# Second-layer tokens stored before their norm, and modulation pieces computed in column groups between stages

## The chip, the cores and the metric

One core of a Trainium2 chip runs the whole program in one launch. The metric is device time in microseconds: three runs gave 3576.17, 3576.55 and 3577.59, median 3576.55. The profile comes from one further execution.

## What is computed

Two transformer blocks on 512 latent tokens of width 1024, all in float32. The first block has two layers and 256 context tokens beside the latent ones; the second block has one layer and is untouched by the change. A layer of the first block:

```python
mod = silu_c @ w_ada[l] + b_ada[l]            # six pieces of 1024
sh1, sc1, gt1, sh2, sc2, gt2 = split(mod, 6)  # modc: the same from c_ctx
h = modulate(rmsnorm(x, g_mix[l]), sh1, sc1)
x = x + gt1 * latent_mixer(h @ w_in[l], ...)  # attention, conv, gates, w_branch, w_out
h2 = modulate(rmsnorm(x, g_ffn[l]), sh2, sc2)
x = x + gt2 * expert_choice_ffn(h2, w_router[l], w_e_gate[l], w_e_up[l], w_e_down[l])
```

`expert_choice_ffn` takes a softmax over 16 experts for every token; each expert then picks its 64 best tokens (32 of the context), applies a gated network of width 1024 and adds the result, times its affinity, to the rows it took. In layer 0 the context tokens go through the same; in layer 1 they only give keys and values.

## The kernel before

Activations lie transposed in SBUF, features on the partitions (8 x 128) and tokens in the free dimension. A dense product takes its weights in blocks of 0.5 MB (`weights`, L86): SP issues the load into `raw`, ScalarE makes a rounded float32r copy `wh` (L95), VectorE the rest `wl` (L96), and TensorE runs three float32r products per block of 128 features (`mm3`, L80, lines L82 to L84). `w` pools hold so many `raw` and so many `wh`/`wl` buffers: 2 and 3 in the latent mixers; 3 and 3 in the context mixer, which has a second pool `w1` with 2 and 2 and takes the two in turn.

**Order.** The stages are: first layer's latent mixer (to about 660 us), context mixer (to 917), first layer's experts (948 to 1600), second layer's latent mixer (to 2180), second layer's experts (2222 to about 2680), second block. In a mixer (`mixer`, L799) dense work and attention are interleaved by hand (`weave`), and at ticks between dense steps a `background` list is advanced (`step`, L411; `period` is the number of ticks per advance). A scheduler then fixes the order on every engine and queue from estimated times, the program's order being its priority, so an instruction that is ready early can stand ahead of earlier ones. Queues then run in order. SBUF of a closed pool is taken over by later ones, tile by tile, and the first user waits for the last reader.

**Modulation.** `first_ada` (L462) computes pieces 0 and 1 of layer 0 at the start in float32: the two condition vectors as 2-column stationary, 256 columns of `w_ada` at a time, with four `wada` buffers; every product is two records in the trace. `ada` (L428) computes the other pieces in the background with split weights: 8 blocks of 0.5 MB a piece, on each four pairs of float32r products (L441, L442), and after every second block a row copy (L444) and two small transposes (L447). The latent mixers do pieces 2 to 5 of their layer, the context mixer pieces 0 and 1 of layer 1. The latent mixer of layer 0 also has `first_gather` (L492), an indirect load into a dummy tile, in its background.

**From w_out to the experts.** During w_out `residual` (L926) makes each 128 features of the new x, and `put` (L963) squares them, scales them by the norm's gain into `u` and adds their part of the router's logits (L970). `ffn_input` (L936) has before that spread the shift `sh2` over all partitions by diagonal products (L954, L955) into `row`. `finish` (L973) sums the squares over features (L979), takes the inverse root on GpSimd (L242), the softmax, and `top_k` (L1019) on VectorE. It then transposes `u` into token rows (L1002), scales them by the norm, adds `row` and writes them to `h2d` in DRAM (L1015). In layer 1 ScalarE scales (L1013) and GpSimd adds (L1014).

**Experts of layer 1** (`last_experts`, L1244) stream 192 blocks of 1 MB (L1269) through 18 buffers, `era` (8) and `erb` (10), on the right side of SBUF where the dense stage's pools lay. The products (`product`, L1265) are float32 with 64 tokens as stationary, the two halves of the columns in the two column groups of TensorE (L1273). `pair` (L1277) gathers the rows of two experts from `h2d` (128 rows, two buffers) and transposes them (L1287). Layer 0's experts (`experts`, L1095) use split weights, five raw buffers, and gather at L1140.

## Time and profile before

| | before |
|---|---|
| median of three runs | 3576.55 us |
| profiled execution | 3583.02 us (span 3581.3) |
| PE busy | 3354.1 us, 94% |
| DVE / ACT / POOL busy | 2268.4 / 1732.4 / 274.4 us |
| granted TensorE clock, mean | 0.977 |
| DMA | 732.9 MB, 205 GB/s over the span |

PE is TensorE's matmuls, DVE VectorE, ACT ScalarE, POOL GpSimd, SP the engine whose queue issues most loads; a "q" behind an engine is its instruction queue. A matmul's recorded length includes its way through the array, so the distance between starts is its price, and a busy PE need not be at its peak.

### The profile page before, as it was taken

The page shows a single profiled execution, that of the slowest core. Times are in us where ns is not written, and L with a number is a line of the kernel's source. Part 1 is how long each engine was busy: PE and PEld are TensorE (multiplying, and loading weights), DVE is VectorE, ACT ScalarE, POOL GpSimd, SP SyncE. Part 2 cuts the span into 40 slices and gives each one's busy share as a digit, 9 for nine tenths or more (in the row PEclk, how much of TensorE's full clock was granted, in tenths as well). Part 3 has the DMA queues.
Part 4 walks back from the last instruction along what each step waited for, and adds up shares of the span by engine and source line. Part 5 has one row for each costly group of instructions (what it writes and reads, how often), then busy time and mean ns, then how long its engine had stood idle before and what let it go on. Part 6 is the DMA issues. An engine that isn't in the chain of part 4 may idle for free. (4 is left out here: it accounts for less than half of the span.)

```text
span 3581.3 us, 46471 instructions
## 1 busy us (share of the span) xinstructions
PE 3354.1 (94%) x17762; PEld 2572.3 (72%) x17762; DVE 2268.4 (63%) x3543; ACT 1732.4 (48%) x2542; POOL 274.4 (8%) x322
## 2 busy tenths in 40 slices
PE   8999999999799999989999996998889999989998
PEld 5787777898688888877777774332228887768887
DVE  4787676588599999977776753232235456854444
ACT  3555554456477777745555542110115355633333
POOL 1101110000200000021011101000001000010000
PEclk9999999999899999989999997999999999999999
DMA  6332437458799999933334376999993432244332
GB/s 218 119 100 93 135 122 220 145 168 239 269 373 335 367 339 341 350 127 95 100 101 130 121 235 255 421 421 421 421 367 103 128 87 88 84 130 138 100 94 83
DMA packets 369227, 732.90 MB, mean 205 GB/s; under 512 B 25534, under 2 KB 262060, under 8 KB 342636
## 3 DMA queue, kind: packets, MB, share of 16 engines
q1 hardware_dynamic: 355728, 695.15, 55.1%
q0 software_dynamic: 7184, 33.31, 2.4%
q8 instruction: 140, 2.29, 0.3%
q10 hardware_dynamic: 6092, 1.47, 0.2%
q14 instruction: 83, 0.68, 0.1%
HBM read 683.71 MB, written 46.14 MB: 204 GB/s over the span
## 5 line engine op out<-in xcount | busy, mean ns | idle before, releaser
L96 DVE TENSOR_TENSOR wl<-raw,wh 128x1024 fp32r<-128x1024 f32 (+2 forms) x423 | 506.6, 1200 | 370.6 <-ACT wh L95 362.9
L95 ACT ACTIVATE wh<-raw 128x1024 fp32r<-128x1024 f32 (+2 forms) x423 | 436.6, 1034 | 490.4 <-PE d L83 301.0
L82 PE MATMUL d<-hh,wh 128*128 128x512 f32 (+1 forms) x1304 | 485.4, 373 | 5.5 <-ACT hh L301 4.3
L83 PE MATMUL d<-hl,wh 128*128 128x512 f32 (+1 forms) x1304 | 484.1, 371 | 1.8 <-DVE hl L302 1.6
L84 PE MATMUL d<-hh,wl 128*128 128x512 f32 (+1 forms) x1304 | 484.3, 372 | 0.4 <-DVE wl L96 0.4
L1116 DVE TENSOR_TENSOR el<-eraw,eh 128x2048 fp32r<-128x2048 f32 x192 | 433.8, 2287 | 33.2 <-ACT eh L1115 32.5
L1115 ACT ACTIVATE eh<-eraw 128x2048 fp32r<-128x2048 f32 x192 | 365.3, 1918 | 105.6 <-PE pup L84 39.3
L82 PEld LDWEIGHTS d<-hh,wh 128*128 128x128 f32 x1304 | 247.6, 190 | 44.1 <-ACT hh L301 5.1
L83 PEld LDWEIGHTS d<-hl,wh 128*128 128x128 f32 x1304 | 247.3, 190 | 39.8 <-DVE hl L302 4.6
L84 PEld LDWEIGHTS d<-hh,wl 128*128 128x128 f32 x1304 | 247.3, 190 | 39.2 <-DVE wl L96 2.3
L642 ACT ACTIVATE prob<-S,st 128x768 f32<-128x768 f32 (+3 forms) x176 | 134.5, 764 | 142.2 <-DVE st L640 66.9
L1332 DVE SCALAR_TENSOR_TENSOR y<-pdn,route,y 64x512 fp32r<-64x512 f32 x32 | 24.0, 750 | 280.6 <-ACT y L1331 280.5
L82 PE MATMUL d<-wh,hh 128*128 128x256 f32 (+1 forms) x528 | 161.2, 305 | 1.9 <-ACT hh L301 1.8
L83 PE MATMUL d<-wl,hh 128*128 128x256 f32 (+1 forms) x528 | 159.9, 303 | 0.3 <-DVE wl L96 0.3
L84 PE MATMUL d<-wh,hl 128*128 128x256 f32 (+1 forms) x528 | 159.7, 303 | 0.2 <-DVE hl L302 0.2
L638 DVE TENSOR_REDUCE st<-S 128x1 f32<-128x768 f32 (+3 forms) x176 | 137.2, 783 | 23.5 <-PE S L703 21.3
L658 ACT ACTIVATE pth<-ppt 128x512 fp32r<-128x512 f32 x184 | 106.0, 595 | 74.8 <-PE ppt L655 71.5
L659 DVE TENSOR_TENSOR ptl<-ppt,pth 128x512 fp32r<-128x512 f32 x184 | 122.6, 685 | 27.2 <-ACT pth L658 26.1
L1273 PE MATMUL pdn<-eraw,at 128*64 128x512 f32 x512 | 119.0, 599 | 21.1 <-DMA eraw<-in_w_e_down 16.4
L655 PE MATMUL ppt<-ident,prob 128*128 128x128 f32 x736 | 121.6, 277 | 7.2 <-DVE prob L647 6.6
L1273 PE MATMUL pup<-eraw,xt 128*64 128x512 f32 x512 | 119.9, 600 | 6.0 <-DMA eraw<-in_w_e_up 6.0
L1273 PE MATMUL pga<-eraw,xt 128*64 128x512 f32 x512 | 118.5, 605 | 2.7 <-DMA eraw<-in_w_e_gate 2.7
(546 smaller groups left out, 7596.4 us busy)
## 6 DMA issues: line engine op xcount, KB each, us to landing
eraw<-in_w_e_gate SPq DMA_DIRECT2D x128, 1024.0 KB
eraw<-in_w_e_up SPq DMA_DIRECT2D x128, 1024.0 KB
eraw<-in_w_e_down SPq DMA_DIRECT2D x128, 1024.0 KB
raw<-in_w_in SPq DMA_DIRECT2D x170, 512.0 KB
raw<-in_w_ada SPq DMA_DIRECT2D x80, 512.0 KB
raw<-in_w_ff SPq DMA_DIRECT2D x64, 512.0 KB
raw<-in_w_out SPq DMA_DIRECT2D x32, 512.0 KB
raw<-in_w_branch SPq DMA_DIRECT2D x48, 256.0 KB
```

The lines of the kernel that those rows point to most:

```text
L82: mm(ps, wh, xh, start=first, stop=False, skip_group_check=skip)
L83: mm(ps, wh, xl, start=False, stop=False, skip_group_check=skip)
L84: mm(ps, wl, xh, start=False, stop=last, skip_group_check=skip)
L95: for ins in (nc.scalar.activation(h[:, :n], raw[:, :n], AF.Copy), nc.vector.tensor_sub(l[:, :n], raw[:, :n], h[:, :n])):
L96: nc.vector.tensor_sub(l[:, :n], raw[:, :n], h[:, :n])):
L638: nc.vector.tensor_reduce(nm, S[:, s0:s1], axis=AX, op=ALU.max, negate=True)
L642: nc.scalar.activation(p, S[:, s0:s1], AF.Exp, bias=nm, accum_out=ls)
L655: nc.tensor.transpose(pt[:, h * 128:h * 128 + 128], probs[h], self.ident)
L659: nc.vector.tensor_sub(pl, pt, ph)
L1115: nc.scalar.activation(h, raw, AF.Copy)
L1116: nc.vector.tensor_sub(lo, raw, h)
L1273: nc.tensor.matmul(ps[halves[j], :], x(k), raw[:, i, j * 512:j * 512 + 512], start=k == 0, stop=k == 7, skip_group_check=True)
```

## The change

Five things. (1) In layer 1 the token rows are transposed and written during w_out, after features 0 to 3 and 4 to 7, unscaled, to a new array `h3d` whose rows have 8 more columns for the norm's factor, written in `finish`; `pair` multiplies by a diagonal of that factor where it transposed before, and adds the shift (loaded as columns through DRAM, in the order in which the layer's features lie) on VectorE. The first two experts' rows are gathered apart, 64 and 64, and there is one gather buffer. (2) Pieces 5 of layer 0, 0 and 1 of layer 1 (after the context mixer's w_out) and 5 of layer 1 (after the latent one's) are made by `ada_between` in float32 with 512 columns in each of two column groups; the latent backgrounds keep pieces 2 to 4 with a period of 4 ticks instead of 3. (3) `first_ada` sets its two pieces side by side in the two column groups. (4) The dummy gather goes, and the context mixer's second weight pool, whose place a pool `z` of five 0.5 MB load buffers takes; in layer 1 the loads use the two `qT` buffers. (5) In layer 1 the pool of `u` lies ahead of the weight pool; the norm's sums take another PSUM tile; one context store moves from POOL's queue to ScalarE's.

```diff
         for q in range(4):
-            for p in (1, 0):
-                ps = self.pd.tile([128, 512], F32, name="d", tag="d")[:2, :256]
-                c0 = p * 1024 + q * 256
-                for ch in range(0, 8, 4):
+            ps = self.pd.tile([128, 512], F32, name="d", tag="d")[:, :256]
+            for ch in range(0, 8, 4):
+                ws = []
+                for p in (1, 0):
                     w = raw[:, n % 4].rearrange("p (k f) -> p k f", k=4)
                     n += 1
+                    c0 = p * 1024 + q * 256
                     nc.sync.dma_start(w, self.A["w_ada"][0][ch * 128:ch * 128 + 512, c0:c0 + 256]
                                       .rearrange("(k p) f -> p k f", p=128))
-                    for k in range(4):
-                        nc.tensor.matmul(ps, self.cs[:, ch + k, :], w[:, k], start=ch + k == 0, stop=ch + k == 7)
-                rows = self.tp.tile([4, 256], F32, name="arow", tag="arow", bufs=1)[:2]
-                nc.scalar.activation(rows, ps, AF.Copy)
-                pt = self.pt.tile([128, 512], F32, name="apt", tag="t")
+                    ws.append(w)
+                for k in range(4):
+                    for h, w in zip((0, 64), ws):
+                        nc.tensor.matmul(ps[h:h + 2], self.cs[:, ch + k, :], w[:, k], start=ch + k == 0,
+                                         stop=ch + k == 7, skip_group_check=True)
...
+                nc.scalar.activation(rows[:2, p * 256:p * 256 + 256], ps[h:h + 2], AF.Copy)
+                for j in range(p * 2, p * 2 + 2):
+                    nc.tensor.transpose(pt[:, j * 2:j * 2 + 2], rows[:2, j * 128:j * 128 + 128], self.ident[:2, :2])
+                self.modulation(0, p, pt[:, p * 4:p * 4 + 4], q * 2, 2)
+            yield
+    def ada_between(self, l, p, raw, banks, row):
+        nc = self.nc
+        ps, pt = banks()
+        k = 0
+        while k < 8:
+            w = raw()
+            n = w.shape[1]
+            nc.sync.dma_start(w, self.A["w_ada"][l][k * 128:(k + n) * 128, p * 1024:p * 1024 + 1024]
+                              .rearrange("(i p) f -> p i f", p=128))
+            for i in range(n):
                 for j in range(2):
-                    nc.tensor.transpose(pt[:, j * 2:j * 2 + 2], rows[:, j * 128:j * 128 + 128], self.ident[:2, :2])
-                c = slice(p * 8 + q * 2, p * 8 + q * 2 + 2)
-                b = lambda a: a[:, None, :].to_broadcast([128, 2, 2])
-                nc.vector.tensor_add(mod[:, :, c], pt[:, :4].rearrange("p (j i) -> p i j", i=2), b(vec[:, c]))
-                if p == 1:
-                    nc.vector.tensor_scalar(mod[:, :, c], mod[:, :, c], 1.0, None, ALU.add)
-                    nc.vector.tensor_mul(mod[:, :, c], mod[:, :, c], b(vec[:, 48 + q * 2:50 + q * 2]))
...
-    def first_gather(self):
-        nc.gpsimd.indirect_dma_start(out=t, out_offset=None, in_=self.A["k_ident"],
-                                     in_offset=bass.IndirectOffsetOnAxis(ap=zero[:, 0:1], axis=0))
...
@@ mixer
         self.do(self.fm(self.A["w_out"][l], 8, 0, 1024, mh, ml, T, residual))
+        between()
         finish()
@@ ffn_input, put, finish
-        row = [self.tp.tile([128, 512], F32, name="brow", tag="hn", bufs=4) for _ in range(2)]
-        for hf in range(2):
+        if l == 1:
+            vec = self.dp.tile([D], F32, name="shift")
+            self.shift = self.cp.tile([128, 8], F32, name="shift", tag="hg")
+            nc.gpsimd.dma_start(vec.rearrange("(k p) -> p k", p=128), B)
+            nc.gpsimd.dma_start(self.shift, vec.rearrange("(c p i) -> p c i", c=4, i=2))
+        row = [self.tp.tile([128, 512], F32, name="brow", tag="hn", bufs=4) for _ in range(2)] if l == 0 else []
+        for hf in range(len(row)):
...
+            if l == 1 and j % 4 == 3:
+                tokens(j // 4)
+        def tokens(hf):
+            for t0 in range(0, nt, 2):
+                tok = self.tp.tile([128, 2, 512], F32, name="tok", tag="big", bufs=2)
+                for t in range(2):
+                    ps = self.pt.tile([128, 512], F32, name="hpt", tag="t")
+                    for j in range(4):
+                        nc.tensor.transpose(ps[:, j * 128:j * 128 + 128],
+                                            u[:, hf * 4 + j, (t0 + t) * 128:(t0 + t) * 128 + 128], self.ident)
+                    ov = tok[:, t].rearrange("t (c i p) -> t c i p", c=2, i=2)
+                    pv = ps.rearrange("t (c p i) -> t c i p", c=2, i=2)
+                    if t == 0:
+                        nc.scalar.activation(ov, pv, AF.Copy)
+                    else:
+                        nc.vector.tensor_copy(ov, pv)
+                nc.gpsimd.dma_start(self.h3d[t0 * 128:t0 * 128 + 256, hf * 512:hf * 512 + 512]
+                                    .rearrange("(t p) f -> p t f", p=128), tok)
         def finish():
-            if lat:
-                ps = self.ps.tile([128, 1024], F32, name="S", tag="S")
-            else:
-                ps = self.ps.tile([128, 512], F32, name="S", tag="Sc", bufs=2)
+            ps = self.pd.tile([128, 512], F32, name="nps", tag="d")
...
+            if l == 1:
+                r8 = self.sp.tile([128, 128], F32, name="r8", tag="diag", bufs=2)[:, :32].rearrange("p (t o) -> p t o", o=8)
+                nc.vector.tensor_copy(r8, r[:, :, None].to_broadcast([128, 4, 8]))
+                nc.gpsimd.dma_start(self.h3d[:, D:].rearrange("(t p) o -> p t o", p=128), r8)
...
                     pass
+            if l == 1:
+                return
...
-                    else:
-                        ov = o.rearrange("t (c i p) -> t c i p", c=2, i=2)
-                        pv, rv = (a.rearrange("t (c p i) -> t c i p", c=2, i=2) for a in (ps, row[hf]))
-                        nc.scalar.activation(ov, pv, AF.Copy, scale=r[:, t:t + 1])
-                        nc.gpsimd.tensor_add(ov, ov, rv)
@@ last_experts
-            def pair(n):
-                xs = xp.tile([128, 1024], F32, name="xs", tag="xs")
-                nc.gpsimd.indirect_dma_start(out=xs, out_offset=None, in_=h2d,
-                                             in_offset=bass.IndirectOffsetOnAxis(ap=gidx[:, n:n + 1], axis=0))
+            first = kp.tile([128, 2], U32, name="gfirst")
+            nc.vector.tensor_copy(first, lat[:, 0, 0:2])
+            def pair(n, alone=False):
+                xs = xp.tile([128, D + 8], F32, name="xs", tag="xs", bufs=1)
                 x = xp.tile([128, 8, 128], F32, name="xt", tag="xt")
-                for hf in range(2):
-                    pt = pm.tile([128, 4, 128], F32, name="ept", tag="d", bufs=5)
-                    for j in range(4):
-                        k = hf * 4 + j
-                        nc.tensor.transpose(pt[:, j], xs[:, k * 128:k * 128 + 128], self.ident)
-                    nc.scalar.activation(x[:, hf * 4:hf * 4 + 4], pt, AF.Copy)
-                return [lambda k, h=h: x[:, k, h] for h in halves]
+                parts = halves if alone else (slice(0, 128),)
+                for i, h in enumerate(parts):
+                    idx = first[:64, i:i + 1] if alone else gidx[:, n:n + 1]
+                    nc.gpsimd.indirect_dma_start(out=xs[h], out_offset=None, in_=self.h3d,
+                                                 in_offset=bass.IndirectOffsetOnAxis(ap=idx, axis=0))
+                for h in parts:
+                    rows = xp.tile([128, 128], F32, name="rows", tag="rows")
+                    nc.vector.tensor_scalar(rows[h, h], self.ident[h, h], xs[h, D:D + 1], None, ALU.mult)
+                    for hf in range(2):
+                        pt = pm.tile([128, 4, 128], F32, name="ept", tag="d", bufs=5)
+                        for j in range(4):
+                            k = hf * 4 + j
+                            nc.tensor.matmul(pt[:, j, h], xs[h, k * 128:k * 128 + 128], rows[h, h], start=True, stop=True)
+                        b = self.shift[:, hf * 4:hf * 4 + 4, None].to_broadcast([128, 4, h.stop - h.start])
+                        nc.vector.tensor_add(x[:, hf * 4:hf * 4 + 4, h], pt[:, :, h], b)
+                    xs_all.extend(lambda k, h=g: x[:, k, h] for g in halves if h.start <= g.start < h.stop)
+                    yield
+            xs_all = []
...
-            xs = pair(0)
+            xs = xs_all
+            two = pair(0, True)
+            next(two)
             pga = acc(pa, "pga")
             run(product(pga, xs[0], A["w_e_gate"][l, 0]))
+            next(two)
...
-                    xs += pair(e // 2 + 1)
+                    next(pair(e // 2 + 1))
@@ open_dense, first_block
         self.tp, self.sp = self.pool(es, "tmp", 2), self.pool(es, "small", 4)
+        if outputs:
+            self.op = self.pool(es, "o")
         if not k:
             self.wps = [(self.pool(es, "w", 3), nraw, nw)]
+        self.h3d = dp.tile([TL, D + 8], F32, name="h3d")
...
-                    self.open_dense(e1)
-                    self.hx, self.op = self.pool(e1, "hx"), self.pool(e1, "o")
+                    self.open_dense(e1, outputs=not first)
+                    self.hx = self.pool(e1, "hx")
+                    if first:
+                        self.op = self.pool(e1, "o")
...
-                    self.background, self.ticks, self.period = [self.ada(l, (2, 3, 4, 5))], -6, 3
-                    if first:
-                        self.background.append(self.first_gather())
-                    xL = self.mixer(l, True, hl, xLd, mLd, gLd, kvc, sink, self.xlp, h2d, 0, xL, arrive())
+                    self.background, self.ticks, self.period = [self.ada(l, (2, 3, 4))], -6, 4
+                    def between():
+                        if first:
+                            return
+                        S = self.ps.tile([128, 1024], F32, name="S", tag="S")
+                        self.ada_between(l, 5, lambda: self.ap.tile([128, 4, TL], F32R, name="zraw", tag="qT", bufs=2)
+                                         .rearrange("p (i a) t -> p i (a t)", i=2).bitcast(F32),
+                                         lambda: [S[:, :512], S[:, 512:]],
+                                         lambda: self.pp.tile([128, 512], F32R, name="zrow", tag="pth").bitcast(F32))
+                    xL = self.mixer(l, True, hl, xLd, mLd, gLd, kvc, sink, self.xlp, h2d, 0, xL, arrive(), between)
...
-                        more = self.pool(e1, "w1"), 2, 2
+                        zp = self.pool(e1, "z", 5, side="right")
                         self.open_dense(e1, nraw=3, nw=3, side="right")
-                        self.wps.append(more)
+                        def between():
+                            for m, p in ((0, 5), (1, 0), (1, 1)):
+                                self.ada_between(m, p, lambda: zp.tile([128, 1, 1024], F32, name="zraw", tag="zraw"),
+                                                 lambda: [self.ps.tile([128, 512], F32, name="S", tag="Sc", bufs=2)
+                                                          for _ in range(2)],
+                                                 lambda: zp.tile([128, 512], F32, name="zrow", tag="zrow", bufs=2))
...
-                        self.background = [self.top_k(True, fp), vectors(), self.load_vectors_2(), self.ada(1, (0, 1))]
+                        self.background = [self.top_k(True, fp), vectors(), self.load_vectors_2()]
                         self.ticks, self.period = -15, 2
                         self.nprob = 8
-                        xC = self.mixer(0, False, [hh, hl], xCd, mCd, gCd, kvc, sink, xcp, h2d, TL)
+                        xC = self.mixer(0, False, [hh, hl], xCd, mCd, gCd, kvc, sink, xcp, h2d, TL, between=between)
                         self.drain()
-                        nc.gpsimd.dma_start(xCd, xC)
+                        nc.scalar.dma_start(xCd, xC)
```

## Rows read from the trace of the kernel before

**Rows 1.** Busy time by stage: us of the stretch, engines' busy us, granted clock, DMA share, GB/s.

```profile
core 0: us, PE busy (x) PEld busy (x) DVE busy (x) ACT busy (x) POOL busy (x), PEclk, DMA share, GB/s
130.00:500.00 370.00, 359.50 (x2100) 289.85 (x2097) 277.25 (x489) 212.82 (x379) 39.69 (x34) 1.00 0.35 109
820.00:882.00 62.00, 59.84 (x481) 54.41 (x482) 49.82 (x98) 42.21 (x77) 2.51 (x2) 1.00 0.86 254
1000.00:1500.00 500.00, 496.14 (x2282) 405.07 (x2281) 471.76 (x312) 373.55 (x254) 14.16 (x11) 1.00 0.94 348
2230.00:2660.00 430.00, 387.99 (x1698) 129.09 (x1696) 117.59 (x178) 47.84 (x76) 4.69 (x5) 1.00 1.01 421
```

**Rows 2.** Modulation products in the context mixer (start us, length us), and the splits' subtraction.

```profile
863.32 0.28 PE L441 MATMUL d<-wh,cst 128*4 128x256 f32 x1
...
865.08 0.28 PE L442 MATMUL d<-wl,cst 128*4 128x256 f32 x1
...
866.52 0.28 PE L447 MATMUL apt<-ident,arow 4*128 4x4 f32 x2 [0.22 <-ACT arow L444]
...
L96 DVE TENSOR_TENSOR wl<-raw,wh 128x1024 fp32r<-128x1024 f32 (+2 forms) x423 | 506.6, 1200 | 370.6 <-ACT wh L95 362.9
```

**Rows 3.** Timeline of the last experts: column-group products, transposes ahead of them.

```profile
2222.18 8.67 PE L1273 MATMUL pga<-eraw,xt 128*64 128x512 f32 x32
...
2576.63 0.99 PE L1287 MATMUL ept<-ident,xs 128*128 128x128 f32 x7
2577.55 5.37 PE L1273 MATMUL pga<-eraw,xt 128*64 128x512 f32 x24
```

**Rows 4.** Timeline of ScalarE in the context mixer: a weight split and what it waited for.

```profile
721.18 1.06 ACT L95 ACTIVATE wh<-raw 128x1024 fp32r<-128x1024 f32 x1 [2.49 <-PE d L83]
```

**Rows 5.** The start: products of the first two pieces, and busy time by stretch.

```profile
53.99 4.48 PE L478 MATMUL d<-wada,cs 128*2 128x256 f32 x20
...
58.61 2.75 PE L478 MATMUL d<-wada,cs 128*2 128x256 f32 x12
...
20.00:55.00 35.00, 31.67 (x178) 16.98 (x177) 16.46 (x37) 12.71 (x22) 2.20 (x3) 1.00 1.05 352
55.00:60.00 5.00, 5.00 (x26) 1.98 (x24) 2.40 (x6) 1.43 (x2) 0.00 (x0) 1.00 0.28 76
```

**Rows 6.** Context joint: last w_out product, gathers, first gathered rows; the stretch's busy time.

```profile
917.30 0.28 PE L84 MATMUL d<-mh,wl 128*128 128x256 f32 x1
...
933.66 7.22 POOL L1140 DMA_INDIRECT xs<-h2d,gidx  x1 [3.97 <-DVE gidx L1092]
...
941.19 0.98 POOL L1140 DMA_INDIRECT xs<-h2d,gidx  x1 [0.30 <-issue]
...
947.76 1.97 PE L1132 MATMUL ept<-ident,xs 128*128 128x128 f32 x8 [17.11 <-DMA xs<-h2d,gidx]
...
917.50:947.50 30.00, 5.70 (x34) 4.57 (x32) 15.58 (x49) 8.96 (x10) 16.23 (x11) 0.57 0.53 201
```

**Rows 7.** Second joint: w_out's last product, first gather, waits of SP and POOL, busy time.

```profile
2179.82 0.39 PE L84 MATMUL d<-mh,wl 128*128 128x512 f32 x1
...
2211.11 1.03 POOL L1280 DMA_INDIRECT xs<-h2d,gpair  x1 [11.03 <-DMA eraw<-in_w_e_down]
...
SPq L1269 <- PE hpt L1002: 14.0, 1, 14.0
...
POOL nrc L242 <- DVE nrc L241: 148.0, 1, 148.0
...
2180.00:2200.00 20.00, 9.35 (x51) 7.47 (x49) 13.70 (x49) 6.56 (x11) 13.34 (x13) 0.61 0.58 219
2220.00:2230.00 10.00, 9.72 (x38) 4.13 (x40) 0.00 (x0) 1.19 (x2) 0.93 (x1) 0.73 0.83 290
```

**Rows 8.** Timeline of a diagonal product ahead of w_out; the page's smallest-packet queue.

```profile
2126.66 0.80 PE L955 MATMUL bps<-diag,ones 128*128 128x128 f32 x2 [2.19 <-DVE diag L954]
...
q10 hardware_dynamic: 6092, 1.47, 0.2%
```

39 lines of the change are left out of this document (28 added, 11 removed).

## The prediction, made before the changed kernel was built

> **What bounds the kernel now.** I read the stage windows first, because the span has stages with different limits. In the first layer's latent mixer and in the part of the context mixer that works on modulation pieces TensorE is busy 97% of the time with its clock granted in full, while DMA stands at 35% in the former [rows 1]. The first layer's experts keep TensorE at 99%, and the second layer's experts keep DMA at 101% with TensorE at 90%, its second latent mixer being like the first. So a microsecond taken off TensorE counts in full in the mixers and in the first layer's experts, and for nothing in the second layer's experts, where only transfer time counts. The places where TensorE stands still are the joints: 917.5 to 947.5 between the context mixer and the first experts (5.7 of 30 us busy), and 2180 to 2222 between the second layer's w_out and its experts (9.4 of the first 20) [rows 6, 7].
>
> **The change part by part**
>
> *Four modulation pieces leave the mixers.* In the old form 16 products of one 256-column block start every 0.117 us (863.32 to 865.08 is 15 steps), and a piece has four such blocks: 64 x 0.117 = 7.5 us. The eight small transposes behind them follow at about 0.1 us each, and each block waits 0.2 to 0.4 us for the row copy [rows 2]; together 9.2 us of TensorE a piece. One piece leaves each latent mixer and two leave the context mixer, which is at 97% while they run [rows 1]. **Minus 9, minus 9, minus 18.** The eight weight splits of a piece go too, 8 x 1.2 = 9.6 us of VectorE; that engine is beside the path and I give it nothing.
>
> *The same pieces come back between the stages.* The nearest row for a float32 column-group product is an expert's: 32 records make one product (two for each float32 call), and 24 of them take 5.37 us, so a pair of records, one for each column group, goes every (5.37 - 0.60)/11 = 0.43 us: 6.9 us for 16 pairs [rows 3]. So a piece still takes 6.9 us plus about 0.9 us of transposes; the saving on TensorE itself is near nothing, and the gain is that the work moves to the joints. Three pieces, 23 us, go into the context joint, where TensorE has 24 us free. Their 24 loads of 0.5 MB are 12.6 MB, 30 us at the 421 GB/s of [rows 1], in a joint whose DMA stands at 53% [rows 6]; five fit into their buffers ahead of time, which leaves 24 us after w_out. The first gathered rows reach TensorE 30 us after w_out ends (917.30 to 947.76), behind norm, top-k and gather [rows 6]. The clock granted there is 0.57, near its lower level of 1.2 GHz, because TensorE stands; with work it comes back, and the first product after the second joint's stand took 8.67 us instead of 6.9, so I count 2 us for that. So both just fit, if the norm's products are not queued behind products that wait for their loads. Bounds: 0 (all hidden) to 20 (the loads queue with the tokens and the gather, and the first product waits for the last piece). I take **plus 6**, nearer to hidden: a gather under full DMA, as in the second layer, needs 11 us from issue (2211.11) to the first product (2222.18) against the 7 after which rows land here, and the token writes ahead of it slow down as well [rows 3, 6, 7].
>
> *The extra weight pool of the context mixer goes,* from five split buffers to three. Now ScalarE's split waits for TensorE to give a buffer back, as at 721.18 [rows 4]: the pool is full and TensorE is never short. With three, two are ready while one is used: 24 products at 0.117 us are 2.8 us a block, so some 5.6 us ahead, against 1.06 us for the split, 1.2 for the subtraction and 1.2 for the load, some 4 us with waits behind other work. Bounds 0 to plus 15; **plus 4**.
>
> *The start.* The first two pieces are 64 float32 calls, 128 records, at one per 0.216 us ((4.48 - 0.38)/19, the last record's own 0.38 taken off), 27.6 us, and in pairs they would take half [rows 5]. But until 55 us DMA is full (1.05), and only afterwards does TensorE work alone [rows 5]. So what counts is the last group of columns, 32 records from 53.99 on, 6.9 us halved, and a little from buffers that come free sooner. Bounds minus 9 to minus 2; **minus 5**. The changeover between a 128-column and a 64-column shape shows no gap: the transposes from 2576.63 last 0.99 us and the products start at 2577.55, before that ends [rows 3]. Against this part speaks the Trainium skill, TensorEngine Tiling (Array Packing), section Key Properties: a change of tiling mode drains the engine. If each of some 16 changeovers cost the 0.16 us by which a record outlasts its pitch, this term would be minus 2 and the total 3 us higher; no gap in the row bears that out.
>
> *The dummy gather goes.* The first real gather takes 7.22 us although the dummy ran before it, and the next 0.98 [rows 6]; so the dummy does not spare it, and I count 0, with plus 6 as the other bound. The Trainium skill, GPSIMD Engine Reference, section Instruction dispatch, gives about 6 us for the first call of freshly loaded code; by it the dummy should have taken that cost away, and the trace has it still there.
>
> *Tokens of the second layer.* Ahead of w_out the eight diagonal products for the shift row and their wait go: TensorE idles 2.19 us there [rows 8], and their 16 records at about 0.11 us are 1.8; **minus 4**. Half of the 32 token transposes come into w_out, 16 x 0.14 (seven in 0.99 us, rows 3) = **plus 2**; their copies lie beside it on ScalarE and VectorE. The other half falls between w_out and the norm, on a chain that gains more than that: GpSimd's adds and the token writes beside and after top-k go, and the gather no longer stands 11 us behind them (2211.11). GpSimd now holds the shift's two small transfers and, behind them, the token writes; it was idle for 148 us up to the norm [rows 7], so neither delays anything. The trace has no row for transfers of 4-byte elements. The nearest is the small queue, 6,092 packets in 0.2% of the 16 engines' span, 7 us [rows 8]: by it the 2,048 small pieces of the shift and the row factors are 2.4 us, and at five times that 12 us, all but a quarter of it beside w_out where DMA has room; I take 0, and the bounds below hold the rest. Scaling by a diagonal, the shift add on VectorE, and a single gather buffer lie under the experts' DMA.
>
> *What the shorter chain is worth.* From w_out's last product at 2179.82 to the first expert product at 2222.18 [rows 3, 7] is 42 us; I expect some 37. But from 2200 on DMA is full until 2660, except 1.7 us at 2220 to 2230 [rows 1, 7], so only bytes and idle DMA count. Idle before that: 8.4 us in 2180 to 2200, where the loads wait 14.0 us for the token transposes [rows 7]; the moved output pool and the earlier transposes give about 8 back. Against it come the last piece's second 2 MB and half the tokens, and two of the eight prefetched expert buffers, which may lie where the piece's q buffers now live on: 3.2 MB net, 7.6 us. **0**, bounds minus 7 to plus 12.
>
> **Sum:** -9 - 9 - 18 + 6 + 4 - 5 - 4 + 2 + 0 = -33 us. The profiled execution took 3583.0 (span 3581.3 and 1.7 around it) and lies 6.5 above the median of 3576.6; so 3550 by its own time and **3544** against the median.
>
> **The rivals**
>
> *The context joint does not hide the three pieces* (0.18). The order of work on an engine is fixed beforehand, so a product that waits for a load holds up the norm behind it. For it: 25 us of loads in a 30 us chain. Against: five buffers ahead and DMA at half. It costs 15 to 20 instead of 6: about 3555. It decides once the pieces' loads end later than the gather's rows land.
>
> *The context mixer starves* (0.11). Three buffers serve blocks of 2.8 us each; with some 60 blocks, 0.4 us each is 24 us: about 3564. Against: the latent mixers run with three as well, but at twice the time a block.
>
> *Slower: the second layer's experts start loading late* (0.09). The last piece's loads reuse the q buffers, and the second two wait for the first products, at w_out's end. If the expert loads that need this memory stand first in SP's queue, all others wait behind them. The 8.4 MB now loaded before 2160 then move behind w_out, 20 us, and DMA idles another 16 to 20 until the piece is done: plus 36 to 40 on a stage where each MB costs 2.4 us. With the rest that is about 3584. It decides once over 33 us of transfer time is lost, which is all eight prefetched loads and 13 us of idle DMA.
>
> *Two-column stationaries do not pair* (0.05). Then the start gains nothing and a piece takes 13.7 us; three are 41 us against 24 free: +5 + 17, about 3566.
>
> *More than I count* (0.06). The joints hide everything and the mixers also run smoother without the splits: about 3520.
>
> **How the numbers follow.** The forecast, 3530 to 3557, holds the remaining 0.51. The range **3520 to 3573** leaves out the slower case and the ends of the starved one and of the large gain. A difference of 0.2% (7 us) is about what a measurement of this kernel can tell from none. Faster by more: forecast, large gain, the joint nearly always, and half of the starved and unpaired cases: 0.82. Within: 0.08. Slower: 0.10.
>
> **What would show it.** Right: both latent mixers about 9 us shorter and the context mixer about 15; the distance from w_out to the first expert's first product in layer one 30 to 40 us, with the pieces inside it; DMA full within 5 us of the second layer's w_out, and its expert stage as long from w_out's end as now (to 2660 about 480 us). Wrong: idle TensorE in the context mixer with VectorE's split as the releaser; the norm's product behind a wait for a piece's load; few expert loads issued before the second w_out ends.

## The result and the profile after

The changed kernel takes **3611.34 us** (median of four runs, 3608.05 to 3614.40) against 3576.36 for the kernel before on the same chip: ratio 1.0097, 95% interval 1.0084 to 1.0109. It is 35 us slower where 33 us less was forecast. The profiled execution took 3610.3 us (span 3608.5, granted clock 0.976). On the chips of the experiments the kernel before stands between 3576 and 3581, so runs are compared by ratio or beside each other.

Where the time went is read from the ends of the stages. The timeline of TensorE and GpSimd after the change (start, length, instruction, idle time before it and its releaser):

```profile
657.23 0.40 PE L84 MATMUL d<-mh,wl 128*128 128x512 f32 x1
677.50 0.58 PE L82 MATMUL d<-wh,hh 128*128 128x256 f32 x1 [6.37 <-ACT wh L95]
...
911.14 0.28 PE L84 MATMUL d<-mh,wl 128*128 128x256 f32 x1
941.40 1.90 POOL L1191 DMA_INDIRECT xs<-h2d,gidx  x1 [7.44 <-issue]
953.85 0.78 PE L82 MATMUL pga<-eh,xth 128*128 128x512 f32 x1
...
2192.11 0.39 PE L84 MATMUL d<-mh,wl 128*128 128x512 f32 x1
2235.86 1.97 PE L1324 MATMUL pga<-eraw,xt 128*64 128x512 f32 x4
```

The first latent stage ends at 657.23, 4.7 us earlier than before (661.9). The context mixer's first product comes 20.3 us behind it, against 1.3 us before (663.19). From there to the last w_out product it is 233.6 us against 254.1, so the context mixer itself gained 20.5. The joint to the first expert's product takes 42.7 us against 32.3 [rows 6]. In the second layer the mixer from the first experts' end to w_out's first product takes 560.4 us against 552.5, w_out itself 52.5 against 56.3, and from w_out's last product to the last expert's last product it is 510.1 against 492.3 [rows 7]. The first experts' stage takes 625.3 us against 621.4, with 17 of the pieces' products still running in it (the last at 957.9, behind the first expert product), and all that lies behind the last expert product is 2.9 shorter. Together these make the 27 us by which the spans of the two profiled executions differ; the medians differ by 35, since the profiled execution of before lies 7 us above its median and that of after 1 below.

Three places in the trace name what is late. First, busy time around the context stage's start (columns as in rows 1), and then SP's wait there (total, times, longest), both after the change:

```profile
660.00:680.00 20.00, 9.16 (x48) 7.29 (x49) 9.80 (x21) 2.58 (x4) 3.25 (x5) 0.64 0.55 187
```

```profile
SPq L92 <- PE hpt L1058: 27.7, 1, 27.7
```

TensorE is busy 9.2 of 20 us (before: 19.0 in the same stretch). SP stood for 27.7 us at the stage's first weight load, until the latent stage's token transposes (hpt) had given back the memory in which the three weight buffers now lie. Before, the first loads went at 603, 610 and 613, during w_out.

Second, the middle of the second latent mixer, timeline of SP, GpSimd, ScalarE and TensorE, and then the busy time of two stretches:

```profile
1922.86 1.27 SPq L92 DMA_DIRECT2D raw<-in_w_branch  x2
...
1932.65 0.76 POOL L981 DMA_DIRECT2D shift<-shift  x1 [9.80 <-DMA shift<-mod]
...
1936.88 1.06 ACT L95 ACTIVATE wh<-raw 128x1024 fp32r<-128x1024 f32 x1 [8.41 <-DMA raw<-in_w_branch]
...
1938.66 0.58 PE L723 MATMUL S<-kT,qT 128*128 128x256 f32 x1 [6.96 <-ACT prob L669]
```

```profile
1924.00:1932.00 8.00, 7.70 (x44) 6.41 (x43) 5.34 (x14) 3.03 (x6) 0.00 (x0) 0.93 0.15 12
1932.00:1936.00 4.00, 0.00 (x0) 0.00 (x0) 0.69 (x1) 0.00 (x0) 3.33 (x4) 0.93 0.77 165
```

The shift's two transfers were not put ahead of w_out, where the code has them, but into the mixer, as soon as their piece was there. GpSimd waited 9.8 us for the landing of the first, 1,024 pieces of 4 bytes, with the rotary work (turning of queries and keys by position) queued behind it. From 1924 to 1932 DMA moves 12 GB/s although a weight load in two parts of 256 KB has been under way since 1922.86; ScalarE gets it at 1936.88, after a wait of 8.41 us, and TensorE, which needs the attention step behind it in ScalarE's queue, stands for 6.96 us.

Third, the expert loads of the second layer, timeline of SP after:

```profile
2195.01 5.42 SPq L514 DMA_DIRECT2D zraw<-in_w_ada  x2
2201.08 5.30 SPq L1320 DMA_DIRECT2D eraw<-in_w_e_gate  x6
```

No expert load goes before 2201.08, behind the last piece's last load; before, eight were issued from 2085.70 to 2151. In the 100 us up to w_out's last product DMA was 51% busy instead of 67%: 16 us of transfer time lost in front of a stage that only transfers bound [rows 1].

### The profile page after: what moved, and what is told of

The parts are those of the page before. It is cut to its first block, busy times and chain, and to the rows that moved or that the text cites. A ratio compares the mean times of both kernels' runs of the same rounds, so it can differ in the third digit from the quotient of the medians.

```text
span 3608.5 us, 46209 instructions
## 1 busy us (share of the span) xinstructions
PE 3370.6 (93%) x17689; PEld 2565.9 (71%) x17698; DVE 2247.1 (62%) x3505; ACT 1687.8 (47%) x2480; POOL 264.4 (7%) x316
## 5 line engine op out<-in xcount | busy, mean ns | idle before, releaser
L96 DVE TENSOR_TENSOR wl<-raw,wh 128x1024 fp32r<-128x1024 f32 (+2 forms) x391 | 465.9, 1194 | 383.5 <-ACT wh L95 381.9
L95 ACT ACTIVATE wh<-raw 128x1024 fp32r<-128x1024 f32 (+2 forms) x391 | 403.3, 1032 | 508.4 <-PE d L83 321.3
L1324 PE MATMUL pdn<-eraw,at 128*64 128x512 f32 x512 | 119.4, 600 | 22.1 <-DMA eraw<-in_w_e_down 18.8
```

Source lines behind the costliest of these rows:

```text
L95: for ins in (nc.scalar.activation(h[:, :n], raw[:, :n], AF.Copy), nc.vector.tensor_sub(l[:, :n], raw[:, :n], h[:, :n])):
L96: nc.vector.tensor_sub(l[:, :n], raw[:, :n], h[:, :n])):
L1324: nc.tensor.matmul(ps[halves[j], :], x(k), raw[:, i, j * 512:j * 512 + 512], start=k == 0, stop=k == 7, skip_group_check=True)
```

## The experiments

### Each late thing undone alone, and the three together

The edits, in this order:

```diff
 (1) -  zp = self.pool(e1, "z", 5, side="right")
        self.open_dense(e1, nraw=3, nw=3, side="right")
     +  zp = self.pool(e1, "z", 5, side="right")
 (2) -  nc.gpsimd.dma_start(vec.rearrange("(k p) -> p k", p=128), B)
     -  nc.gpsimd.dma_start(self.shift, vec.rearrange("(c p i) -> p c i", c=4, i=2))
     +  for i2 in range(2):
     +      for h in range(2):
     +          nc.tensor.matmul(pb[h * 64:h * 64 + 64, i2 * 4:i2 * 4 + 4], even[:, i2], halves[:, h],
     +                           start=True, stop=True, skip_group_check=True)
     +  nc.vector.tensor_copy(self.shift.rearrange("p (c i) -> p i c", i=2),
     +                        pb[:, :8].rearrange("p (i c) -> p i c", c=4))
 (3) -  [self.ada(l, (2, 3, 4))], -6, 4
     +  [self.ada(l, (2, 3, 4) if first else (2, 3, 4, 5))], -6, 4 if first else 3
```

In (2), even holds the identity's columns by parity and halves the even and odd columns of the shift B. In (3) the second layer has no work between w_out and the norm, and its latent mixer is back at every third tick.

> The changed kernel, with one edit: in the context stage the pool of the pieces' loads is opened behind the weight buffers, so that the weight buffers lie where they lay before the change. Theory (the stage's first weights wait for the memory that the latent stage's token tiles still hold, 27.7 us of waiting in front of the first weight load): the first context product comes back from 677.5 to about 663 after w_out's end at 657, and the whole kernel is 12 to 15 us faster than the changed one, about 3597. Rival (the delay comes from the missing pair of early weight buffers, wherever the others lie): the first product stays near 675 and the time within 3 us of 3611.

> The changed kernel, with one edit: the shift column of the second layer's tokens is put in order by four small products and a copy instead of two transfers of 1,024 pieces of 4 bytes. Theory (the transfers hold up a weight load and GpSimd's rotary work at 1922 to 1938 of the trace): the idle 7.0 us of TensorE there and the slow clock behind it go, the second latent mixer is 8 to 10 us shorter and the kernel comes to about 3602. Rival (the mixer lost its time to the other order in which the pieces' products now fall among the attention units): the gap moves elsewhere, the time stays within 3 us of 3611.

> The changed kernel, with one edit: the second layer's last modulation piece goes back into the mixer's background (four pieces, every third tick) and nothing stands between w_out and the norm there. Theory A (the piece's later loads stand ahead of the expert loads in SP's queue and in the expert buffers' memory, and wait for products behind w_out): eight expert loads are issued before w_out ends again, and the stretch from w_out's last product to the last expert product falls from 510 to some 492 us; against it the mixer pays 9 us for the piece; the kernel comes to about 3600. Theory B (the expert loads are held up by the output pool's new place or by the tokens' tiles): the first expert load stays at w_out's end, and the kernel gets 5 to 9 us slower, about 3618.

> The three edits of the runs beside it together. If each theory holds and they add up: 14 + 9 + 10 off the changed kernel, about 3578, which is the time before the change. If the rivals hold: between 3605 and 3615.

| | median | ratio to before (95%) |
|---|---|---|
| (1) weights under the pieces' pool | 3598.84 | 1.0047 (1.0030 to 1.0064) |
| (2) shift by products | 3605.42 | 1.0069 (1.0053 to 1.0086) |
| (3) last piece in the background | 3597.29 | 1.0046 (1.0030 to 1.0063) |
| all three | 3571.04 | 0.9977 (0.9967 to 0.9987) |

Against the changed kernel's 1.0097 the edits take off, by ratio times some 3578 us, 18, 10 and 18 us, each known to some 7 us, and 43 together: the theories hold, (1) and (3) with more than was forecast (12 to 15 and some 11), and nearly add up. The first context product in (1), from the timeline:

```profile
662.59 0.58 PE L82 MATMUL d<-wh,hh 128*128 128x256 f32 x1
```

The wait for the token transposes is now that of the pieces' loads (SP's waits in (1)):

```profile
SPq L514 <- PE hpt L1058: 30.1, 1, 30.1
```

And SP's first expert load in (3):

```profile
2107.05 0.35 SPq L1320 DMA_DIRECT2D eraw<-in_w_e_gate  x1
```

In (1) the stage starts 6 us after the latent one, 14 sooner than in the changed kernel, and the first experts' stage takes 621.8 us again. The 3 to 5 us that are missing to the 1.3 of before stay in every version with the new place of the norm's sums, also with the context part undone (4.4 and 4.9 us; the two runs are below); without it the start is at 0.9 to 1.3. TensorE with the context part undone and in the kernel before:

```profile
658.95 1.43 PE L1035 MATMUL nps<-ones,acc 128*128 128x1 f32 x8
...
660.35 0.56 PE L82 MATMUL d<-wh,hh 128*128 128x256 f32 x1
```

```profile
663.19 0.39 PE L82 MATMUL d<-wh,hh 128*128 128x256 f32 x1
...
665.43 1.03 PE L979 MATMUL S<-ones,acc 128*128 128x1 f32 x8
```

The first product now stands behind the norm's sums, where before it went ahead of them. That the sums share the products' PSUM tiles since the change would explain it; no run tests that.

In (3) expert loads go out during w_out (last product 2198.8), DMA in its last 100 us is back at 70%, and the stretch from w_out's last product to the last expert's takes 490.8 us; with all three edits it is 492.6, as before the change. So the tokens and the output pool's new place cost nothing there; the piece between w_out and the norm does. (The mixer of (3), at the old pace but with the shift's transfers still in it, is no shorter, 563.4 us; with four pieces and without the transfers it is 553.3. Other pairs of traces with and without them differ by 6 and 12 us.)

### The piece's loads on another queue

Base: edits (1) and (2), whose gains leave some 3589. The four loads of the second layer's last piece are issued by GpSimd (`nc.gpsimd` for `nc.sync` in ada_between).

> The changed kernel with the first two of the three edits (weight buffers under the pieces' loads, shift by products), the second layer's last piece still between w_out and the norm, but its four loads issued by GpSimd instead of SP. Theory A (the third and fourth load, which wait for the first products, stand ahead of the expert loads in SP's queue): the first expert loads are issued during w_out again, near 2085, at least the two whose buffers don't overlap those of the piece, and the kernel is some 5 us below the sum of the two edits (3589), about 3584. Theory B (every expert load waits for the memory that the piece's tiles hold): the first expert load stays at w_out's end and the kernel within 3 us of 3589.

3591.76 us, ratio 1.0031 (1.0019 to 1.0044): theory B's number. W_out's last product and SP's first expert load, and then what SP waited for:

```profile
2168.78 0.39 PE L84 MATMUL d<-mh,wl 128*128 128x512 f32 x1
...
2175.80 1.46 SPq L1326 DMA_DIRECT2D eraw<-in_w_e_gate  x3
```

```profile
SPq L1326 <- PE hpt L1021: 20.7, 1, 20.7
...
SPq L1326 <- PE S L518: 3.6, 1, 3.6
SPq L1326 <- PE S L526: 2.2, 1, 2.2
```

With nothing of the piece in SP's queue the first expert load still comes 7 us behind w_out. So the piece's loads in SP's queue do not explain it alone. What does stays open: the load first in line waited for token transposes, which delay no load in (3), and only later ones waited for the piece's products (3.6 and 2.2 us). That the piece's tiles hold the memory of the expert buffers that were loaded first before, so that others come to stand first in line, fits; other memory for these tiles was not tried.

### What a background piece and its pace cost

The change also lets a piece advance at every fourth tick instead of every third. Base: the version with three edits, except for the last run, which has edits (1) and (2) and the piece between w_out and the norm.

```diff
-  [self.ada(l, (2, 3, 4) if first else (2, 3, 4, 5))], -6, 4 if first else 3
+  [self.ada(l, (2, 3, 4))], -6, 4
```

This is the piece left out at the new pace; the runs at the old pace end in "4 if first else 3", the one with the first layer's piece put back has (2, 3, 4, 5) at pace 3 in both layers and two pieces in the joint, and the last one has

```diff
-  [self.ada(l, (2, 3, 4))], -6, 4
+  [self.ada(l, (2, 3, 4))], -6, 3
```

> The version with three edits, with the second layer's last modulation piece left out altogether and filled with zeros (so that part of the output isn't computed), three pieces at every fourth tick as in the changed kernel. Theory of the prediction (a piece in the background costs the latent mixer 9 us): the second latent mixer falls from 553 to about 544 us, the kernel to about 3562. Rival (a piece in the background fills gaps that the attention chain leaves, and its removal only uncovers them): the mixer stays within 3 us of 553 and the kernel within 3 us of 3571.

> The version with three edits, with the second layer's last piece left out and filled with zeros (that part of the output isn't computed), but the other three at every third tick as with four pieces. Theory (the piece only fills gaps): the second latent mixer stays within 3 us of 553, the kernel within 3 us of 3570. Rival (the removal saves 9 us, and the wider spacing of every fourth tick lost them again): the mixer falls to about 545, the kernel to about 3562.

> The version with three edits without the second layer's last piece (filled with zeros, so that part of the output isn't computed), three pieces at every third tick, beside the version with the piece on the same chip. Theory of the prediction (a piece costs the mixer 9 us): 7 to 11 us below it. Rival (it fills gaps): within 3 us.

> The version with three edits, with the first layer's last piece back in its latent mixer's background (four pieces, every third tick), so that two pieces instead of three stand in the context joint. Theory of the prediction (9 us for the piece in the mixer, and only part of 8 us for it in the joint): the mixer is 9 us longer, the joint 4 to 8 us shorter, together about 3574. Rival (a background piece is nearly free): the mixer within 3 us, the joint 5 to 8 us shorter, about 3564.

> The changed kernel with the first two of the three edits (weight buffers under the pieces' loads, shift by products), and the three pieces of both latent mixers at every third tick as before the change, not at every fourth. Without the pace, the run with the other queue for the piece's loads stands for this version (3592, second latent mixer 556 us from the experts' end to w_out's first product). Theory (the wider pace cost what the missing piece saved): the second latent mixer falls to 545 to 548 us, the kernel to 3580 to 3585. Rival (the pace is nothing, the piece filled gaps): the mixer stays within 3 us of 555, the kernel at 3589 to 3595.

Second latent mixer, from the experts' end to w_out's first product, in us:

| | pace | pieces | mixer | ratio to before (95%) |
|---|---|---|---|---|
| three edits | 3 | 4 | 553.3 | 0.9977 (0.9967 to 0.9987) |
| the same again | 3 | 4 | 553.4 | 0.9975 (0.9965 to 0.9986) |
| piece left out | 4 | 3 | 553.9 | 0.9975 (0.9966 to 0.9984) |
| piece left out, old pace | 3 | 3 | 546.0 | 0.9951 (0.9938 to 0.9965) |
| the same again | 3 | 3 | 545.8 | 0.9969 (0.9957 to 0.9981) |
| (1) and (2), other queue | 4 | 3 | 556.0 | 1.0031 (1.0019 to 1.0044) |
| (1) and (2), old pace | 3 | 3 | 544.8 | 0.9984 (0.9975 to 0.9993) |

At the old pace a piece costs the mixer 7.5 us, near the forecast 9, of which w_out gives 1.5 to 4 back. The whole run is 9 and 2 us shorter by ratio in the two pairs, the second not clear of noise and short of the forecast 7 to 11. At the new pace its removal gives nothing. So where nothing but the pace differs, it costs the second mixer 8 us. The first mixer agrees: w_out's last product falls at 648.9 at the old pace, in the one run that has it with three pieces, and at 654.7 in the run above it, at 653.6 to 660.3 in all 12 with the new one. The last two rows differ by 0.0047, **17 us (11 to 22) for the pace** in both mixers, 6 in the first and 11 in the second. They differ in the queue of the piece's loads too, which gave nothing above. The last run (3571.85) is faster than its forecast, 3580 to 3585, which counted the second mixer alone. Busy time of the second mixer, new pace, then old:

```profile
1560.00:2116.00 556.00, 529.62 (x2983) 430.47 (x2984) 393.45 (x695) 294.16 (x529) 71.81 (x63) 0.98 0.37 115
```

```profile
1557.00:2101.00 544.00, 527.31 (x2980) 427.85 (x2979) 393.96 (x695) 293.88 (x529) 66.71 (x61) 0.99 0.37 117
```

The products are the same in number (some records are missing) and nearly in busy time; idle falls from 26.4 to 16.7 us, spread over a dozen waits of 0.2 to 7 us. The small transposes of a piece, for one, waited 3.8 us for ScalarE's row copy at the new pace and 0.2 at the old. Why the pieces fall worse among the attention units at every fourth tick stays open. Putting the first layer's last piece back, at the old pace, shortens the context joint by 2.8 us and lengthens the mixer by 2.3: 3568.11, ratio 0.9969 (0.9956 to 0.9981), no clear difference from 0.9977 and neither of the two forecasts.

### Where else the context pieces could go

Base: three edits. The first run has

```diff
-        between()
         finish()
+        between()
```

for the context stage; the second puts all three pieces into the first latent mixer at every second tick; the third restores the context stage of before (extra pool, two pieces in the mixer, four in the first latent one, there at the old pace).

> The version with three edits (weight buffers under the pieces' loads, shift by products, last piece of the second layer in the background; 3571), with one edit more: in the context stage the norm, top-k and the tokens are written out ahead of the three pieces instead of behind them. Theory (the context joint, 42 us from w_out's last product to the first expert's product against 32 before the change, is long because the pieces' loads stand ahead of the residual's loads in SP's queue and their products ahead of the norm's on TensorE): the joint falls to 34 to 38 us and the kernel to about 3565. Rival (it is long because the gathered rows have to land while DMA is full with the pieces' 12.6 MB, whatever the order): the joint stays at 40 or more, 3569 to 3575, or it moves to the first expert's loads.

> The version with three edits, with all three pieces of the context joint put into the background of the first layer's latent mixer instead (six pieces there, every second tick; nothing stands between w_out and the norm any more, the pieces' pool goes). Theory (the latent mixer's attention chain leaves gaps that pieces fill, as leaving one out gave nothing): the latent mixer is up to 6 us longer, the context joint falls from 42 to the 32 us it had before the change, the kernel comes to about 3564. Rival (TensorE's time is what counts in the mixer, and the one piece left out was a special case): 3 x 9 us more in the mixer, 10 less in the joint, about 3586.

> The version with three edits, with the context part undone: the extra weight pool and two pieces in the context mixer, four in the first latent mixer, nothing in the joint. What is left of the change is the start in pairs, the second layer's tokens and the missing dummy gather. From the rows (context mixer 18 us longer, joint 10 shorter): about 3578, 8 above the version with three edits. Rival (the context part gives nothing on balance): within 3 us of 3570.

Norm first: joint 42.3 us, 3568.40, ratio 0.9972 (0.9961 to 0.9983); the order is not what makes it long, the rival stands. Six in the latent mixer: its w_out ends 42 us later, the joint takes 25.0, 3599.02, ratio 1.0054 (1.0040 to 1.0067); the rival again, and by more than 27 (the pace of two ticks is in this, too). Context as before: **3565.49, ratio 0.9951** (0.9938 to 0.9965), below 0.9977. Neither number fits: the part does not gain 8 us, by ratio it costs 9. The context mixer is 18.6 us longer (254.9 against 236.3), but the joint takes 23.2 us, against 42.3 with the pieces and against 32.3 in the kernel before. What had become of the 9 us between these two?

### The gather beside VectorE's subtractions

GpSimd's first gathers and VectorE's subtractions for the first expert's weights (el), context as before:

```profile
932.03 1.05 POOL L1197 DMA_INDIRECT xs<-h2d,gidx  x1 [3.53 <-DVE gidx L1149]
933.39 2.03 POOL L1197 DMA_INDIRECT xs<-h2d,gidx  x1 [0.31 <-issue]
...
932.31 4.48 DVE L1173 TENSOR_TENSOR el<-eraw,eh 128x2048 fp32r<-128x2048 f32 x2
```

Here the gather starts 0.28 us ahead of the subtractions and takes 1.05 us. In the kernel before, it starts at 933.66, just behind the start of three subtractions, and takes 7.22 us [rows 6]; VectorE's timeline there:

```profile
933.28 6.69 DVE L1116 TENSOR_TENSOR el<-eraw,eh 128x2048 fp32r<-128x2048 f32 x3
```

The edit holds the subtractions back until the gather is issued:

```diff
  nc.scalar.activation(h, raw, AF.Copy)
+ if early and c < 3:
+     self.tc.keep_in_program_order(nc.gpsimd.memset(lo[:, 0, 0:1].bitcast(F32), 0.0))
  nc.vector.tensor_sub(lo, raw, h)
```

It is early for the first expert's first product alone, and the write is pinned behind the gather on GpSimd.

> The version with three edits once more, as the measure for the runs beside it on the same chip: 0.997 to 0.998 of the kernel before.

> The version with three edits, with one edit more: VectorE's first three subtractions for the first expert's weights are held until GpSimd has issued the first gather (GpSimd writes one element of their output behind the gather). Theory (the gather stands still while VectorE subtracts: in the trace it starts 7.58 us after GpSimd's last work and only when two of three subtractions of 2.24 us are over, and in the run with the context part undone, where it started 0.3 us ahead of them, it took 1.05 us): the gather is issued within 1.5 us of its indices, 3 to 5 us earlier, and the joint falls from 42 to 37 to 39 us; the kernel 3 to 5 us below the version with three edits. Rival (the gather has a first-call cost of some 7 us, or its rows land late because DMA is full anyway): the gather's time or its landing move by under 1.5 us and the time is the same.

> The version with three edits, the context part undone as in the run with that name, and the first gather held ahead of the subtractions as in the run beside it, so that the two differ in the context part alone. Theory A (the part gives nothing: its mixer's 18 us come back in a joint that is 19 us longer, 42 against 23): within 3 us of the run beside it. Theory B (the context part pays 8 us and the run with it undone was lucky in its gather): 5 to 10 us slower than the run beside it. Theory C (it costs): more than 3 us faster.

> The kernel before, its dummy gather kept, with one edit: VectorE's first three subtractions for the first expert's weights are held until GpSimd has issued the first gather. Theory (the gather stands still while VectorE subtracts two operands side by side): the first gather takes 1 us instead of 7.22, its rows land some 6 us earlier, the context joint falls from 32 to 25 or 26 us and the kernel is 5 to 7 us faster than before. Rival (7.22 us are the first call's own, or the dummy's doing): the gather still takes about 7 us, the time stays within 2 us.

In the kernel before, with its dummy gather kept:

```profile
931.10 1.04 POOL L1142 DMA_INDIRECT xs<-h2d,gidx  x1 [3.81 <-DVE gidx L1092]
932.13 0.18 POOL L1117 MEMSET el<- 128x1 f32 x3
932.47 2.96 POOL L1142 DMA_INDIRECT xs<-h2d,gidx  x1 [0.16 <-issue]
...
932.28 4.49 DVE L1118 TENSOR_TENSOR el<-eraw,eh 128x2048 fp32r<-128x2048 f32 x2 [1.48 <-POOL el L1117]
```

7.22 becomes 1.04, the joint falls from 32.3 to 22.1 us, the kernel to 3565.29, ratio **0.9969** (0.9959 to 0.9980): this one edit gives the kernel before 11 us, where 5 to 7 were forecast. Besides the gather's own 6 us, its rows land 3.3 us after its end instead of 6.8. On the version with three edits the same edit gives nothing (3572.35, 0.9982, 0.9973 to 0.9991, against 0.9975 beside it). The gather takes 1.05 us there too, but goes late for another reason:

```profile
933.61 1.05 POOL L1199 DMA_INDIRECT xs<-h2d,gidx  x1 [7.63 <-DMA zraw<-in_w_ada]
```

By the profile it waited for a load of the pieces, up to 933.6; the token rows that it reads had landed only at 932.5 themselves, 7.1 us after their store was issued at 925.41 (2.9 to 3.0 without the pieces). Its rows then took 7.5 us to reach TensorE with DMA full; the joint is 40.2 us. With the context part undone and the gather first, 3563.21, ratio 0.9958 (0.9945 to 0.9972), 9 us below the run beside it: theory C. Two runs without the context part (0.9951, 0.9958) stand against four with it (0.9972 to 0.9982), some 8 us apart: the joint pays 16 to 20 us for the pieces, about what the mixer gains, and where the rest goes the traces, whose spans lie 0.5 us apart in one pair and 15 in the other, don't settle.

### The start alone

The kernel before with the paired first pieces and nothing else of the change.

> The kernel before, with one part of the change alone: the first two modulation pieces as products of two column groups side by side. By the prediction's term the kernel is 5 us (2 to 9) faster than before. Rival: the latent mixer behind it takes the gain back, within 2 us of before.

3574.07, ratio 0.9987 (0.9978 to 0.9996): 4.5 us, the forecast 5. The pairs, from TensorE's timeline of the changed kernel:

```profile
37.27 0.28 PE L83 MATMUL S<-wl,hh 128*128 128x256 f32 x1
37.48 1.89 PE L481 MATMUL d<-wada,cs 128*2 128x256 f32 x14
```

## Why the prediction was wrong

The sum was -33. Four steps of it failed: the pace, which had no term (17 us); the extra pool's term, +4, which left out what the pools' new places do to a stage's start (some 18); the shift's transfers, at 0 (10); and the shorter chain with its late expert loads, at 0 (18).

- **The start, -5:** right, -4.5. In the changed kernel 14 records of the pairs take 1.89 us, that is, without the last one's own 0.38, a pair every 0.216 us, where one record went before [rows 5]. The Trainium skill's rule on draining at a change of tiling mode (TensorEngine Tiling (Array Packing), section Key Properties) would, by the prediction's estimate, have left 2 us; the interval, 1.4 to 7.9, does not exclude that. The prediction saw no gap at a change; there is one of 0.09 us (2577.35 to 2577.55 between starts where transposes follow every 0.11), but the products of the start begin 0.21 us behind a block's product, and the next one 0.31 behind them, in either form, so a change to pairs costs nothing more.
- **Pieces out of the latent mixers, -9 and -9:** right in size at the old pace (the first mixer's end 5.6 to 9.3 us earlier than in four runs with the start in pairs and the piece still in it, the second mixer 7.7 shorter than before), and the step that failed is one left out: the diff moves the pace from 3 to 4, and the prediction gave that no price. It takes back 17.
- **Pieces out of the context mixer, -18, and the extra pool, +4:** -20.5 together in the changed kernel, -14 forecast (-16 to -19 in the later versions), so the pool's going starves nothing in mid-stage. But the term looked for its price in the wrong place. Where the weight buffers lie decides when the stage may begin to load, and that cost 14 us at the stage's start and 3.5 in the experts behind it, 18 by the ratio of edit (1). Its own upper bound, 15, was meant for starving. The 3 to 5 us at the start that edit (1) does not give back had no term either, and their cause is not shown.
- **The context joint, +6:** +10.4 in the trace, inside its bounds. The comparison was flawed underneath: 10 us of the joint before were the gather's collision, so the pieces really cost 16 to 20, what the rival in which the joint does not hide them had as 15 to 20. The part as a whole, forecast at -8, gives nothing or costs.
- **The dummy gather, 0:** right, but from a wrong reading: the 7.22 us that the dummy did not spare were VectorE's subtractions beside the gather, and no cost of its own. Without the dummy the first gather takes 1.05 us, with it 1.04, once the subtractions are out of the way. The first-call cost of the Trainium skill (GPSIMD Engine Reference, section Instruction dispatch) shows in no run here.
- **Tokens, -4 and +2 in w_out:** right in most: w_out takes 52.4 to 54.2 us in 14 of the 17 traces with them and 54.8 to 56.3 in the three without, but 55.3 to 57.9 in three with them.
- **The shift's transfers, 0:** wrong. "it was idle for 148 us up to the norm [rows 7], so neither delays anything" took the place from the code; the transfers went into the mixer, 10.5 and 5.9 us long, ahead of GpSimd's rotary work, and with a weight load stalled beside them. 10 us (edit 2). The upper bound of 12 us was right in size; that it lies beside w_out was not.
- **What the shorter chain is worth, 0 with -7 to +12:** wrong; +18 (edit 3). Of eight prefetched loads I let two be late. All eight were: the rival "the second layer's experts start loading late", given 0.09, came about, with 16 to 18 us instead of 36 to 40, because DMA did not stand idle afterwards (busy share 1.01 from 2200 to 2240). Which memory or order holds them back is not settled; that the piece between w_out and the norm does it is shown.

So -33, +17 for the pace, +17 for late weights, +10 for the shift, +18 for the late expert loads and +4 in the joint make +33; measured +35. With each term known to 5 to 7 us, and those last 3 to 5 of the stage's start not in it, that they meet so closely is luck. The first three are things that the change sets in the diff itself: a period, a pool's place, a queue; for the late expert loads it may be a buffer's tag.

## What to carry to other kernels

Work that is moved to a joint should bring its own memory: ask of each tile in it which later load lies on the same bytes (shown here for the context stage, likely for the second layer's experts), and of each pool that is taken away what lies under its neighbour. Give every number that a diff changes a term of its own, a pacing constant too. And before work is put into a gap, find out why the gap is there: here 10 of its 32 us went away by holding back three VectorE instructions (ratio 0.9969 by that alone), which is more than the gap was worth as a hiding place.

## What the runs showed of the hardware

- GpSimd's gather does not get through while VectorE subtracts two SBUF operands: 7.22 us beside three such subtractions of 2.3 us, 2.03 to 4.28 where a second gather runs beside two, 0.96 to 1.05 with none. In all 20 traces a gather of the first experts that begins beside a subtraction ends 0.8 to 0.95 us after the end of one, though not always of the next; two that began 0.3 us ahead of the subtractions took 1.05. The Trainium skill has a rule for it (Trainium Architecture — The Big Picture, section What this means for kernel authors: VectorE and GpSimd share a port, under an exclusive lock); these numbers agree with it.
- A transfer of 4 KB in pieces of 4 bytes took 10.5 us from issue to landing, and the weight load issued beside it some 13 us, with DMA at 12 GB/s between.
